# Block pairs' seven products in another order: four with rows of the first half of the tokens, then three of the second

## The chip, the cores and the metric

The kernel runs on one core of one Trainium2 chip. The metric is the device time of one execution in microseconds. Three runs of the kernel before gave 1287.32, 1287.40 and 1286.79 us, median 1287.32.

## The reference

One layer of a streaming encoder over 576 tokens (512 of a new stream, 64 of a running one), in float32. What matters here are the two feed-forward layers and the output projection of branch B.

```python
def swiglu_ffn(x, w_gate_up, w_down):
    gate, up = jnp.split(x @ w_gate_up, 2, axis=-1)
    return (jax.nn.silu(gate) * up) @ w_down
...
x = x + 0.5 * swiglu_ffn(rms_norm(x, ffn1_norm), ffn1_w_gate_up, ffn1_w_down)
...
y_b = b_act @ w_b_out
...
x = x + 0.5 * swiglu_ffn(rms_norm(x, ffn2_norm), ffn2_w_gate_up, ffn2_w_down)
```

The model width is 1024 and the hidden width 2816, that is 22 hidden tiles of 128.

## The kernel before

Features lie on the 128 partitions, the tokens on the free axis, in two halves of 288. Every float32 operand of a product is split into a high part (rounded to the format that TensorE multiplies at full rate) and a low part (the rest), and a product is three matmuls: high by high, high by low, low by high.

Most hidden tiles are computed as block pairs. The gate and the up weights of a hidden tile (in branch B two neighbouring output tiles), cut along the contraction into two parts of four tiles, and the two halves of the tokens form a 2 by 2 block product. It is done with seven products instead of eight, in Winograd's form: `plan_block` plans the weights, among them four sums s1 to s4 of weight blocks; `Forms` makes the sums t1 to t4 of the activations; `operands` lists the activations in the order of the products. A product (`block`) is 12 matmuls of 288 columns, into one bank of PSUM. Two products that follow each other share a PSUM tile of two banks (`bank`, line 171); the pool has four such tiles, and the pairing of banks runs on from pair to pair until `spare.clear()` at the end of a group. There are 41 block pairs: 18 in ffn1, 21 in ffn2 and 2 in branch B. In the feed-forward layers they stand in groups (four groups a layer, of one to six pairs), and a group ends with the down projection of its hidden tiles; the first two down tiles run interleaved (`both`).

TensorE multiplies an operand of the first half of the tokens or of the second. The halves start at addresses that differ by 128 bytes modulo 256, and `ws.places` puts the high and low parts of a product's weights at matching offsets: `(SHIFT, 0)` for products of the second half, `(0, SHIFT)` for those of the first.

The weights come through `Stream`. Each product has a unit; `lead` (called by `get` ahead of each product) works ahead by six units. For a unit it makes a sum if one is due (`add`, VectorE), writes the high part (`begin`, ScalarE) and the low part: VectorE subtracts it (`end`), or, for `how == "dma"`, ScalarE writes minus the high part and POOL issues a DMA that adds the raw weights to it. In a pair the units on a11, a12 and a22 go the second way in nearly all cases, the four sums the first. The raw weights are loaded by SP into six buffers.

While product n + 1 is issued, `steps[n]` combines what product n has given: `q1` is a copy of product 0 by ScalarE, `u2`, `u3` and `u4` are sums on VectorE, `t` becomes the gate and `cu` the up part. `gate` multiplies `t` by `R`, the reciprocal root of the norm, and ScalarE takes the Silu. `up`, `hidden` and `parts` of a pair run with the first products of the next (`rest`). Each engine keeps the order in which the code issues its instructions (`Ordered`). All of their instructions are issued through one helper, line 90.

Of the kernel before, what the change touches and what calls it, by code (L numbers as in the profile page):

```python
# [22 lines left out]
KU = KT // 2  # L23
# [90 lines left out]
def tile_encoder_step(  # L114
# [66 lines left out]
    def half(ap, s):  # L181
        return ap[:, s * H : (s + 1) * H]
# [176 lines left out]
    def plan_block(name, raws, homes, lows=("dma", "dma", "dma")):  # L359

        a21, a22, a11, a12 = raws
        s1, s2, s3, s4 = ((name, n) for n in range(1, 5))
        plan[name] = [
            ws.unit(src, KU, home, how, sums)
            for home, (src, how, sums) in zip(homes, (
                (a11, lows[0], ((s1, (a21, a22)),)),
                (s2, "dve", ((s2, (s1, a11)),)),
                (s1, "dve", ()),
                (s3, "dve", ((s3, (a11, a21)),)),
                (a12, lows[1], ()),  # L370
                (s4, "dve", ((s4, (s2, a12)),)),
                (a22, lows[2], ()),
            ))
        ]
        for n, unit in enumerate(plan[name]):
            second = n in (1, 5, 6)
            ws.places[unit] = (SHIFT, 0) if second else (0, SHIFT)

    def plan_ffn(f, gu, dn):
# [295 lines left out]
    class Forms:  # L675
# [25 lines left out]
        def operands(self, xg):  # L701

            first, second = (
                [(half(hi, s), half(lo, s)) for hi, lo in xg] for s in range(2)
            )
            t1, t2, t3, t4 = (
                [(half(hi, s), half(lo, s)) for hi, lo in (self.parts[p][i] for p in range(KU))]
                for i in range(2) for s in range(2)
            )
            return first[:KU], t2, t1, t3, first[KU:], second[KU:], t4  # L710


    ss = Sum()
# [140 lines left out]
    def ffn(f, xg, sums, finish, forms, R=None, todo=()):  # L854
        todo = list(todo)

        rest = []


        def plain(i, hs):  # L860
            nonlocal R
            t, up = ttile(), (f, "u", i)
            ps = product((f, "g", i), xg, order=IN_TURN if f == "f2" and i == 0 else None)
            got = None if up in early else chunks(up)
            if R is None:
                R = rstd(sums)
            ups = product(up, xg, got=got)
            hs.append(None)
            at = len(hs) - 1

            def gate():
                dve.tensor_tensor(halves(t), ps, halves(R), op=ALU.mult)
                sca.activation(t, t, AF.Silu)

            def hidden():
                dve.tensor_tensor(halves(t), ups, halves(t), op=ALU.mult)
                hs[at] = high(t)

            def parts():
                hs[at] = hs[at], low(t, hs[at])  # L880

            if f == "f2":
                rest.extend((gate, hidden, parts))
                return
            gate()
            forming()
            hidden()
            forming()
            parts()
            forming()  # L890

        def forming():
            if todo:
                for step, p in todo.pop(0):
                    step(p)

        def pair(i, hs, last):
            qu, uu, t, cu = (ttile() for _ in range(4))
            q1, u2, u3, u4 = half(qu, 0), half(qu, 1), half(uu, 0), half(uu, 1)
            q = []  # L900

            def q7():
                dve.tensor_tensor(u3, q[3], u2, op=ALU.add)
                dve.tensor_tensor(half(cu, 1), u3, q[2], op=ALU.subtract)

            def gate():
                dve.tensor_tensor(half(t, 1), q[5], u4, op=ALU.add)
                dve.tensor_tensor(t, t, R, op=ALU.mult)
                sca.activation(t, t, AF.Silu)

            steps = (
                lambda: sca.copy(q1, q[0]),
                lambda: dve.tensor_tensor(u2, q[1], q1, op=ALU.subtract),
                lambda: dve.tensor_tensor(u4, q[2], u2, op=ALU.subtract),
                q7,
                lambda: dve.tensor_tensor(half(t, 0), q[4], q1, op=ALU.add),
                gate,
            )
            for n, xs in enumerate(bs):
                q.append(block(ws.get(plan[f, "s", i][n]), xs))  # L920
                if n > 0:
                    steps[n - 1]()
                if rest:
                    rest.pop(0)()

            hs.append(None)
            at = len(hs) - 1

            def up():
                if last:  # L930
                    dve.tensor_tensor(t, t, R, op=ALU.mult)
                dve.tensor_tensor(half(cu, 0), q[6], u3, op=ALU.add)

            def hidden():
                dve.tensor_tensor(cu, cu, t, op=ALU.mult)
                hs[at] = high(cu)

            def parts():
                hs[at] = hs[at], low(cu, hs[at])

            rest.extend((up, hidden, parts))

        for g, grp in enumerate(GROUPS):
            hs = []
            for i in grp:
                if i < PLAIN[f]:
                    plain(i, hs)
                    continue
                if i == PLAIN[f]:
                    ws.ahead = AHEAD_UNITS  # L950
                    bs = forms.operands(xg)
                pair(i, hs, grp[-1] == FT - 1)
            while rest:
                rest.pop(0)()
            spare.clear()
            if grp[-1] < FT - 1:
                for j, ps in enumerate(both([(f, "d", g, j) for j in range(2)], hs, turn=True)):
                    update(j, ps, R)
                for j in range(2, KT):
                    update(j, product((f, "d", g, j), hs), R)  # L960
            else:
                finish(g, hs)
# [315 lines left out]
    def block_pair(i):  # L1278
# [2 lines left out]
        q1, u2, u3, u4 = half(qu, 0), half(qu, 1), half(uu, 0), half(uu, 1)  # L1281
        q = []

        def second():
            dve.tensor_tensor(u3, q[3], u2, op=ALU.add)
            dve.tensor_tensor(half(c2, 1), u3, q[2], op=ALU.subtract)

            if i == KU - 1:
                MS[4], MS[5] = split(M[4]), split(M[5])

        def first():
# [1 line left out]
            dve.tensor_tensor(c1, c1, SGB[j], op=ALU.mult)  # L1293
            merged(j, c1)

        steps = (
            lambda: sca.copy(q1, q[0]),
            lambda: dve.tensor_tensor(u2, q[1], q1, op=ALU.subtract),
            lambda: dve.tensor_tensor(u4, q[2], u2, op=ALU.subtract),
            second,  # L1300
            lambda: dve.tensor_tensor(half(c1, 0), q[4], q1, op=ALU.add),
            first,
        )
        for n, xs in enumerate(bs):
            q.append(block(ws.get(plan["yb", "s", i][n]), xs))
            if n > 0:
                steps[n - 1]()
        dve.tensor_tensor(half(c2, 0), q[6], u3, op=ALU.add)
        dve.tensor_tensor(c2, c2, SGB[j + 1], op=ALU.mult)
# [166 lines left out]
```

## Time and profile before

| | |
|---|---|
| median of three runs | 1287.32 us |
| profiled execution | 1287.41 us |
| its span | 1285.6 us |
| granted TensorE clock, mean | 0.998 |
| TensorE busy | 1275.0 us, 99% |
| VectorE busy | 927.8 us, 72% |
| ScalarE busy | 762.8 us, 59% |
| POOL busy | 357.2 us, 28% |
| matmuls | 9728 |
| 41 block pairs, 11.05 us each | about 453 us |

The page gives busy time per engine as a share of the span and, in another part, the chain of work that ended last. A matmul's row shows its whole passage (293 ns on the mean) although the next one starts 0.13 us later, so the distance between starts says more than the duration. A row of the list in order of time has the start in us, the duration, the engine, the line, what is written and read, and, in brackets, how long the engine was idle before it and who ended that. `PE` is TensorE, `DVE` VectorE, `ACT` ScalarE.

### The profile page before, as it was taken

To read this page: it belongs to the slowest core of one execution; us is meant where nothing else is said; L and a number is where in the kernel's file an instruction comes from. 1 tells how busy PE (TensorE), PEld (TensorE's weight loads), DVE (VectorE), ACT (ScalarE), POOL (GpSimd) and SP (SyncE) were. 2 spreads that over 40 slices of the span, in tenths; PEclk is the share of its full clock that TensorE was granted. 3 is DMA by queue.
4 is the path that set the end of the run, shared out by engine and by line. 5 is a ranking of instruction groups with operands and counts; after the bars stand their busy time and mean duration, and the time that the engine had idled before them with its cause. 6 is when DMAs were issued, how large, how long until landed. Compare 5 with 4: busy or idle time off the path is not lost.

```text
span 1285.6 us, 25688 instructions
## 1 busy us (share of the span) xinstructions
PE 1275.0 (99%) x9728; PEld 1273.3 (99%) x9728; DVE 927.8 (72%) x1544; ACT 762.8 (59%) x1354; POOL 357.2 (28%) x455
## 2 busy tenths in 40 slices
PE   9999999999999999999999999999999999999997
PEld 9999999999999999999999999999999999999996
DVE  6868668748846998888895166756967848847955
ACT  7645646646776645555444576467665655654664
POOL 0032332332333444333321221122142141241230
PEclk9999999999999999999999999999999999999999
DMA  7287786886799898878885767686597696796693
GB/s 222 69 181 154 164 181 154 178 183 147 157 225 230 173 207 166 172 168 177 169 169 124 170 137 160 147 207 147 132 177 174 147 203 147 165 207 140 153 181 93
DMA packets 286091, 213.94 MB, mean 166 GB/s; under 512 B 15376, under 2 KB 248848, under 8 KB 285968
## 3 DMA queue, kind: packets, MB, share of 16 engines
q0 software_dynamic: 55440, 91.12, 43.3%
q1 hardware_dynamic: 228784, 120.35, 32.9%
q8 instruction: 77, 1.26, 0.4%
q10 hardware_dynamic: 1744, 0.83, 0.2%
q14 instruction: 46, 0.38, 0.1%
HBM read 116.17 MB, written 4.98 MB: 94 GB/s over the span
## 4 chain that ended last, share of the span: by engine, by line
PE 98%; DMA 1%; DVE 0%; ACT 0%; SPq 0%; DVEq 0%; issue 0%
PE mm L90 98%; DMA x<-in_x_dram 0%; DMA gains<-in_params_dram 0%; DVE g L90 0%; DVE tmp L90 0%; SPq L730 0%; DVE act L90 0%; ACT act L90 0%; DVEq L1466 0%; DVE r L90 0%; DVE x L90 0%; ACT tmp L90 0%; ACT r L90 0%
## 5 line engine op out<-in xcount | busy, mean ns | idle before, releaser
L90 PE MATMUL mm<-act,u 128*128 128x288 f32 x4758 | 666.2, 293 | 0.0
L90 PEld LDWEIGHTS mm<-act,u 128*128 128x128 f32 x4758 | 637.2, 188 | 0.0
L90 PE MATMUL mm<-act,g 128*128 128x288 f32 x3030 | 431.5, 293 | 0.0
L90 PEld LDWEIGHTS mm<-act,g 128*128 128x128 f32 x3030 | 408.9, 188 | 0.3 <-DMA g<-raw 0.2
L90 POOL DMA_DIRECT2D u<-raw x194 | 169.3, 873 | 477.1 <-ACT u L90 311.6
L90 PE MATMUL mm<-act,act 128*128 128x288 f32 (+2 forms) x1896 | 258.8, 293 | 0.5 <-DVE act L90 0.3
L90 PEld LDWEIGHTS mm<-act,act 128*128 128x128 f32 x1896 | 251.1, 188 | 1.1 <-DVE act L90 0.6
L90 ACT CAST u<-raw 128x512 fp32r<-128x512 f32 (+2 forms) x207 | 118.9, 575 | 172.3 <-PE mm L90 142.0
L90 POOL DMA_DIRECT2D g<-raw x124 | 107.8, 869 | 302.5 <-ACT g L90 246.4
L90 DVE SCALAR_TENSOR_TENSOR w<-g,prm,w 128x606 f32<-128x606 f32 x232 | 179.3, 842 | 1.4 <-ACT w L90 1.4
L90 DVE TENSOR_TENSOR tmp<-mm,tmp 128x288 f32<-128x288 f32 (+1 forms) x251 | 112.7, 457 | 67.3 <-PE mm L90 50.9
L90 ACT ACTIVATE u<-u 128x512 fp32r<-128x512 f32 (+2 forms) x194 | 115.0, 593 | 6.2
L90 ACT CAST g<-raw 128x512 fp32r<-128x512 f32 (+2 forms) x136 | 75.1, 552 | 45.6 <-DMA raw<-in_ffn_w_down_dram 16.3
L90 DVE SCALAR_TENSOR_TENSOR tmp<-mm,r 128x576 f32<-128x576 f32 x48 | 36.3, 756 | 74.8 <-PE mm L90 74.8
L90 POOL DMA_DIRECT2D act<-raw x67 | 59.1, 883 | 107.9 <-ACT act L90 94.2
L90 ACT CAST act<-tmp 128x576 fp32r<-128x576 f32 x92 | 61.9, 675 | 43.6 <-DVE tmp L90 42.5
L90 ACT CAST g<-w 128x512 fp32r<-128x512 f32 x79 | 49.0, 620 | 63.4 <-DVE w L90 55.8
L90 ACT CAST u<-w 128x512 fp32r<-128x512 f32 x81 | 50.2, 619 | 59.5 <-DVE w L90 43.3
L90 DVE TENSOR_TENSOR act<-tmp,act 128x576 fp32r<-128x576 f32 x92 | 67.5, 754 | 18.4 <-ACT act L90 16.8
L90 ACT ACTIVATE g<-g 128x512 fp32r<-128x512 f32 (+2 forms) x124 | 70.9, 572 | 3.9
L90 DVE TENSOR_TENSOR w<-raw,raw 128x512 f32<-128x512 f32 x82 | 56.1, 684 | 16.6 <-DMA raw<-in_ffn_w_gate_up_dram 12.1
L90 ACT ACTIVATE tmp<-tmp 128x576 f32<-128x576 f32 x47 | 32.2, 685 | 44.1 <-DVE tmp L90 44.1
(86 smaller groups left out, 833.4 us busy)
## 6 DMA issues: line engine op xcount, KB each, us to landing
raw<-in_ffn_w_gate_up_dram SPq DMA_DIRECT2D x171, 256.0 KB, 3.4
u<-raw POOLq DMA_DIRECT2D x137, 256.0 KB, 4.1
raw<-in_w_in_dram SPq DMA_DIRECT2D x112, 256.0 KB, 3.9
raw<-in_ffn_w_down_dram SPq DMA_DIRECT2D x96, 192.0 KB, 3.8
g<-raw POOLq DMA_DIRECT2D x67, 256.0 KB, 4.0
act<-raw POOLq DMA_DIRECT2D x61, 256.0 KB, 4.3
g<-raw POOLq DMA_DIRECT2D x43, 192.0 KB, 4.5
u<-raw POOLq DMA_DIRECT2D x41, 192.0 KB, 4.5
```

The source lines that it names most:

```text
L90: return self.tc.keep_in_program_order(fn(*args, **kwargs))
```

## The change

The products of a pair come in another order. Before: a11, s2, s1, s3, a12, s4, a22; after: a11, s1, s3, a12, s2, s4, a22. In the first order products 1, 5 and 6 multiply rows of the second half of the tokens, in the second one products 4, 5 and 6. The combining steps follow: nothing is computed behind products 1 and 2; `t`'s first half comes behind product 3, and u2, u4, u3 and the lower half of `cu` together behind product 4 (`middle`). In branch B the splits of `M[4]` and `M[5]` go with them.

```diff
             for home, (src, how, sums) in zip(homes, (
                 (a11, lows[0], ((s1, (a21, a22)),)),
-                (s2, "dve", ((s2, (s1, a11)),)),
                 (s1, "dve", ()),
                 (s3, "dve", ((s3, (a11, a21)),)),
                 (a12, lows[1], ()),
+                (s2, "dve", ((s2, (s1, a11)),)),
                 (s4, "dve", ((s4, (s2, a12)),)),
                 (a22, lows[2], ()),
             ))
...
-            second = n in (1, 5, 6)
+            second = n >= 4
             ws.places[unit] = (SHIFT, 0) if second else (0, SHIFT)
...
-            return first[:KU], t2, t1, t3, first[KU:], second[KU:], t4
+            return first[:KU], t1, t3, first[KU:], t2, second[KU:], t4
...
-            def q7():
-                dve.tensor_tensor(u3, q[3], u2, op=ALU.add)
-                dve.tensor_tensor(half(cu, 1), u3, q[2], op=ALU.subtract)
+            def middle():
+                dve.tensor_tensor(u2, q[4], q1, op=ALU.subtract)
+                dve.tensor_tensor(u4, q[1], u2, op=ALU.subtract)
+                dve.tensor_tensor(u3, q[2], u2, op=ALU.add)
+                dve.tensor_tensor(half(cu, 1), u3, q[1], op=ALU.subtract)
...
-            steps = (
-                lambda: sca.copy(q1, q[0]),
-                lambda: dve.tensor_tensor(u2, q[1], q1, op=ALU.subtract),
-                lambda: dve.tensor_tensor(u4, q[2], u2, op=ALU.subtract),
-                q7,
-                lambda: dve.tensor_tensor(half(t, 0), q[4], q1, op=ALU.add),
-                gate,
-            )
+            steps = {
+                0: lambda: sca.copy(q1, q[0]),
+                3: lambda: dve.tensor_tensor(half(t, 0), q[3], q1, op=ALU.add),
+                4: middle,
+                5: gate,
+            }
             for n, xs in enumerate(bs):
                 q.append(block(ws.get(plan[f, "s", i][n]), xs))
-                if n > 0:
+                if n - 1 in steps:
                     steps[n - 1]()
```

`block_pair` (branch B) changes in the same way.

VectorE's order in one pair of ffn1, before. `act` is the low half of the previous hidden tile, `mm` are products (two share a number), `w` are sums of weights, `g` and `u` the low parts of weights; `tmp_3094` holds q1 and u2, `tmp_3095` u3 and u4, `tmp_3096` is t, `tmp_3097` is cu:

```order
L90 TENSOR_TENSOR tmp_3094<-mm_3112,tmp_3094 128x288
L90 TENSOR_TENSOR act_3165<-tmp_2948,act_3146 128x576
L90 TENSOR_TENSOR g_3149<-w_3126,g_3148 128x512
L90 TENSOR_TENSOR w_3168<-raw_3019,raw_2958 128x512
L90 TENSOR_TENSOR tmp_3095<-mm_3151,tmp_3094 128x288
L90 TENSOR_TENSOR u_3172<-w_3099,u_3172 128x512
L90 TENSOR_TENSOR tmp_3095<-mm_3151,tmp_3094 128x288
L90 TENSOR_TENSOR tmp_3097<-tmp_3095,mm_3151 128x288
L90 TENSOR_TENSOR g_3189<-w_3168,g_3188 128x512
L90 TENSOR_TENSOR w_3207<-w_3126,raw_3106 128x512
L90 TENSOR_TENSOR tmp_3096<-mm_3191,tmp_3094 128x288
L90 TENSOR_TENSOR tmp_3096<-mm_3191,tmp_3095 128x288
```

The same engine and pair now:

```order
L90 TENSOR_TENSOR act_3166<-tmp_2948,act_3144 128x576
L90 TENSOR_TENSOR g_3151<-w_3099,g_3150 128x512
L90 TENSOR_TENSOR u_3169<-w_3146,u_3169 128x512
L90 TENSOR_TENSOR w_3184<-w_3099,raw_2999 128x512
L90 TENSOR_TENSOR tmp_3096<-mm_3153,tmp_3094 128x288
L90 TENSOR_TENSOR w_3205<-w_3184,raw_3106 128x512
L90 TENSOR_TENSOR tmp_3094<-mm_3191,tmp_3094 128x288
L90 TENSOR_TENSOR tmp_3095<-mm_3112,tmp_3094 128x288
L90 TENSOR_TENSOR tmp_3095<-mm_3153,tmp_3094 128x288
L90 TENSOR_TENSOR tmp_3097<-tmp_3095,mm_3112 128x288
L90 TENSOR_TENSOR u_3207<-w_3184,u_3207 128x512
L90 TENSOR_TENSOR tmp_3096<-mm_3191,tmp_3095 128x288
```

u2, which stood ahead of the low half `act`, and u4 have moved behind product 4 (`mm_3191`), in one run of four operations with u3 and cu.

ScalarE's order in the same pair, before, from the Silu on (`CAST` writes a high part, the `ACTIVATE` behind it minus the high part for a DMA, `COPY` is q1):

```order
L90 ACTIVATE tmp_2947<-tmp_2947 128x576
L90 CAST g_3101<-raw_2810 128x512
L90 ACTIVATE g_3102<-g_3101 128x512
L90 CAST u_3128<-raw_3019 128x512
L90 ACTIVATE u_3128<-u_3128 128x512
L90 COPY tmp_3094<-mm_3112 128x288
L90 CAST act_3146<-tmp_2948 128x576
L90 CAST g_3148<-w_3126 128x512
L90 CAST u_3172<-w_3099 128x512
L90 CAST g_3188<-w_3168 128x512
L90 CAST u_3209<-raw_3106 128x512
L90 ACTIVATE u_3209<-u_3209 128x512
```

And now:

```order
L90 ACTIVATE tmp_2947<-tmp_2947 128x576
L90 CAST g_3101<-raw_2810 128x512
L90 ACTIVATE g_3102<-g_3101 128x512
L90 CAST u_3126<-raw_2999 128x512
L90 ACTIVATE u_3126<-u_3126 128x512
L90 COPY tmp_3094<-mm_3112 128x288
L90 CAST act_3144<-tmp_2948 128x576
L90 CAST g_3150<-w_3099 128x512
L90 CAST u_3169<-w_3146 128x512
L90 CAST g_3186<-raw_3106 128x512
L90 ACTIVATE g_3187<-g_3186 128x512
L90 CAST u_3207<-w_3184 128x512
```

The first seven stand where they stood; a12 (`raw_3106`) has moved ahead of a sum.

More of the change, by code (lines that the diff above doesn't have):

```diff
@@ L1282, in block_pair, with middle @@
         q = []
-        def second():
-            dve.tensor_tensor(u3, q[3], u2, op=ALU.add)
-            dve.tensor_tensor(half(c2, 1), u3, q[2], op=ALU.subtract)
+        def middle():
+            dve.tensor_tensor(u2, q[4], q1, op=ALU.subtract)
+            dve.tensor_tensor(u4, q[1], u2, op=ALU.subtract)
+            dve.tensor_tensor(u3, q[2], u2, op=ALU.add)
+            dve.tensor_tensor(half(c2, 1), u3, q[1], op=ALU.subtract)
             if i == KU - 1:
@@ L1294, in first @@
             merged(j, c1)
[L1296 to L1303, printed above, removed]
+        steps = {
+            0: lambda: sca.copy(q1, q[0]),
+            3: lambda: dve.tensor_tensor(half(c1, 0), q[3], q1, op=ALU.add),
+            4: middle,
+            5: first,
+        }
         for n, xs in enumerate(bs):
             q.append(block(ws.get(plan["yb", "s", i][n]), xs))
-            if n > 0:
+            if n - 1 in steps:
                 steps[n - 1]()
```

## The prediction

> **What bounds the kernel now.** I read the page first, then the chain that ended last, then one pair's instructions in order of time on each engine, then single DMA issues.
>
> ```profile
> span 1285.6 us, 25688 instructions
> ...
> PE 1275.0 (99%) x9728; PEld 1273.3 (99%) x9728; DVE 927.8 (72%) x1544; ACT 762.8 (59%) x1354; POOL 357.2 (28%) x455
> ...
> PE 98%; DMA 1%; DVE 0%; ACT 0%; SPq 0%; DVEq 0%; issue 0%
> ```
>
> TensorE is the chain: 98% of the span, one matmul behind the other. So an edit can gain only by making matmuls follow each other more closely, and it can lose by making TensorE wait for a weight or a bank. The profiled execution took 1287.41 us: its span of 1285.6 and 1.8 around it. The median is 1287.32, so I take 0.1 off at the end. A measurement of this kernel tells about 0.2% (2.6 us) from no change.
>
> TensorE's rows of one pair in ffn2, the third of its group (start, us, then what; twelve matmuls a product; I number the products 0 to 6):
>
> ```profile
> 1002.70 1.75 PE L90 MATMUL mm<-act,g 128*128 128x288 f32 x12
> ...
> 1007.44 1.74 PE L90 MATMUL mm<-act,u 128*128 128x288 f32 x12
> 1009.01 1.74 PE L90 MATMUL mm<-act,g 128*128 128x288 f32 x12
> ...
> 1012.17 1.74 PE L90 MATMUL mm<-act,g 128*128 128x288 f32 x12
> 1013.75 0.42 PE L90 MATMUL mm<-act,u 128*128 128x288 f32 x2
> ```
>
> From start to start a pair takes 11.05 us, a product 1.58, a matmul 0.131. Only product 3 (1007.44 to 1009.01, 1.57) has neighbours on both sides that multiply the same half of the tokens. TensorE does not wait within the pair.
>
> VectorE's rows there. `tmp<-tmp,r` is the step in `gate` that multiplies by R; I call its start the R step. The row 1007.53 is u2, 1008.10 the low half of the previous hidden tile, 1010.95 and 1011.43 are u3 and the lower half of cu, 1013.01 the two halves of t:
>
> ```profile
> 1003.38 0.76 DVE L90 TENSOR_TENSOR tmp<-tmp,r 128x576 f32<-128x576 f32 x1
> ...
> 1007.53 0.46 DVE L90 TENSOR_TENSOR tmp<-mm,tmp 128x288 f32<-128x288 f32 x1 [0.55 <-ACT tmp L90]
> 1008.10 0.76 DVE L90 TENSOR_TENSOR act<-tmp,act 128x576 fp32r<-128x576 f32 x1
> 1008.78 0.69 DVE L90 TENSOR_TENSOR g<-w,g 128x512 fp32r<-128x512 f32 x1
> ...
> 1010.95 0.45 DVE L90 TENSOR_TENSOR tmp<-mm,tmp 128x288 f32<-128x288 f32 x1
> 1011.43 0.45 DVE L90 TENSOR_TENSOR tmp<-tmp,mm 128x288 f32<-128x288 f32 x1
> 1011.80 0.68 DVE L90 TENSOR_TENSOR g<-w,g 128x512 fp32r<-128x512 f32 x1
> 1012.40 0.68 DVE L90 TENSOR_TENSOR w<-w,raw 128x512 f32<-128x512 f32 x1
> 1013.01 0.81 DVE L90 TENSOR_TENSOR tmp<-mm,tmp 128x288 f32<-128x288 f32 x2
> 1013.85 0.76 DVE L90 TENSOR_TENSOR tmp<-tmp,r 128x576 f32<-128x576 f32 x1
> ```
>
> VectorE goes from one R step to the next in 10.47 us with hardly a gap, in a pair of 11.05: it is almost a second bound. Start to start, an operation that needs the one before it follows after 0.48 (1010.95 to 1011.43), one that doesn't after 0.37 (1011.43 to 1011.80), one behind 512 columns after 0.60 (1011.80 to 1012.40), one behind the low half after 0.68.
>
> The R step drives the rest. ScalarE waits for it with the Silu, and behind the Silu stand in its queue the splits of two weights that a DMA on POOL finishes:
>
> ```profile
> 1004.18 0.69 ACT L90 ACTIVATE tmp<-tmp 128x576 f32<-128x576 f32 x1 [1.47 <-DVE tmp L90]
> 1007.39 0.68 ACT L90 CAST act<-tmp 128x576 fp32r<-128x576 f32 x1
> 1006.33 0.86 POOL L90 DMA_DIRECT2D g<-raw  x1 [4.30 <-DVE w L90]
> 1007.50 0.86 POOL L90 DMA_DIRECT2D u<-raw  x1 [0.31 <-ACT tmp L90]
> ```
>
> From the R step it is 0.80 to the Silu, 2.95 and 4.12 to the two DMAs (a22 of this pair, a11 of the next), 4.01 to the high half of the hidden tile and 4.72 (1008.10) to its low half. A later R step makes these weights later by as much.
>
> **The change: what it saves.** A pair's seven products change the half of the tokens four times before (into 1, into 2, into 5, into the next pair) and twice after. Four changes touch eight product ends. With 1.57 for a product without one, 7 x 1.57 = 10.99, and the 0.06 left to 11.05 over eight ends is 0.0075 an end, so two changes less are 0.03 us a pair. The rows round to 10 ns, which leaves 0.01 to 0.05. The starts behind them, read to the nanosecond, give 1.5733 for that product and 11.054 for the pair, which is 0.005 an end and 0.021 a pair. I take 0.021: 41 pairs x 0.021 = 0.85 us, with 0.4 and 2.0 as ends.
>
> The Trainium skill's page "TensorE: Matmul & The Clock Gate" (Part 2, step by step) says that TensorE has two independent read ports in SBUF, and that loading the next weights takes no bandwidth from the running matmul. By that rule the half of the tokens would not matter, the saving would be 0 instead of 0.85, and the sum below 1290.2. The rows above disagree by a hundredth of a microsecond a product, and the measurement decides.
>
> **What it moves.** The number of instructions stays, and so do their sizes: the same four sums, splits and DMAs a pair, seven combining operations, loads on SP in the same order. SP's loads are not moved past anything; the a12 load must be there one product earlier, and ScalarE reaches a12 only 5.7 us behind the R step, and waits for no load there in the rows of before: I cost it nothing. On POOL the a12 DMA comes one earlier in the pair, with its product, behind the same two DMAs: nothing. Banks: product 1 is now held until product 4 is done; the first products behind a group that ends on an odd pair reuse those of products 2 and 3, which are read 0.05 us before they are needed. I cost that nothing and keep 0.5 us for five such places as an end.
>
> What costs is VectorE's order. u2 and u4, which stood in the slack behind products 1 and 2, now stand behind product 4 with u3 and cu. Two things follow.
>
> First, u2 waits for more. Two products share a PSUM tile, and an operation that is issued behind the next product waits for that one too, if it writes the same tile. Two rows show this:
>
> ```profile
> 990.06 1.74 PE L90 MATMUL mm<-act,g 128*128 128x288 f32 x12
> 990.27 0.82 DVE L90 TENSOR_TENSOR tmp<-mm,tmp 128x288 f32<-128x288 f32 x2
> 991.12 0.76 DVE L90 TENSOR_TENSOR tmp<-tmp,r 128x576 f32<-128x576 f32 x1
> 1018.76 0.46 DVE L90 TENSOR_TENSOR tmp<-mm,tmp 128x288 f32<-128x288 f32 x1 [1.31 <-PE mm L90]
> ```
>
> In the first pair of that group, and every second one from there (call them odd), products 4 and 5 share a tile: the step on product 4 started at 990.27, just when product 5 had ended (product 6 starts at 990.06), and the R step came 0.85 later. The pair began 6 x 1.58 earlier, at 980.59, so its R step is at 10.5. In the even pairs 1 and 2 share one, and u2 there waited 1.31 us for product 2 (1018.76; the pair starts at 1013.75). After the change u2 stands where the step on product 4 stood: in odd pairs it starts at 9.68 at the earliest, then u4 0.48, u3 0.37, cu 0.48, a weight's low half 0.37, t 0.60, the R step 0.48 later: 9.68 + 2.78 = 12.46 us into the pair.
>
> Second, VectorE's loop gets longer: 4.72 from the R step to the low half, then 0.68 + 0.60 + 0.60 + 0.60 (two low halves, a sum, t's first half) + 0.37 + 0.60 (a sum, u2) + 2.78 = 10.95, against 10.47. That is still 0.1 below the 11.03 of a pair, so the even pairs' R step is at 12.46 + 10.95 - 11.03 = 12.37 and the odd ones keep 12.46.
>
> **Where this reaches TensorE.** At the end of a group the first weights of the second down tile are read ten matmuls, 1.31 us, behind the last pair; their DMA follows the R step of the last pair but one. There are seven such ends with DMAs. The first, the tightest and the costliest (R step; POOL issue; its landing; TensorE's first matmul behind the pair):
>
> ```profile
> 144.01 0.76 DVE L90 TENSOR_TENSOR tmp<-tmp,r 128x576 f32<-128x576 f32 x1
> 150.49 0.86 POOL L90 DMA_DIRECT2D g<-raw  x1
> g<-raw POOLq DMA_DIRECT2D x1, 192.0 KB, 4.5
> 154.37 2.40 PE L90 MATMUL mm<-act,g 128*128 128x288 f32 x17
> 939.45 0.76 DVE L90 TENSOR_TENSOR tmp<-tmp,r 128x576 f32<-128x576 f32 x1
> 945.92 0.86 POOL L90 DMA_DIRECT2D g<-raw  x1
> g<-raw POOLq DMA_DIRECT2D x1, 192.0 KB, 4.2
> 948.72 3.06 PE L90 MATMUL mm<-act,g 128*128 128x288 f32 x20
> 1122.48 0.76 DVE L90 TENSOR_TENSOR tmp<-tmp,r 128x576 f32<-128x576 f32 x1
> 1129.17 0.86 POOL L90 DMA_DIRECT2D u<-raw  x1
> u<-raw POOLq DMA_DIRECT2D x1, 192.0 KB, 4.8
> 1133.42 2.81 PE L90 MATMUL mm<-act,u 128*128 128x288 f32 x20
> ...
> u<-raw POOLq DMA_DIRECT2D x137, 256.0 KB, 4.1
> ...
> u<-raw POOLq DMA_DIRECT2D x1, 256.0 KB, 5.9
> ```
>
> - 154.37: the weights land at 154.99, read at 155.68: 0.69 to spare. The R step (two pairs before the end, so 144.01 - 154.37 + 22.11 = 11.75) moves to 12.37: 0.62 later, no stall.
> - 948.72: they land at 950.12 and should be read at 950.03: nothing to spare. The R step there is at 12.84; this group comes late out of the mixer, and before it catches up by 11.05 - 10.47 a pair, which the longer loop no longer does. Two loops of 10.95 for 10.47 make it 0.96 later; in one of the two pairs a22 is split without a DMA, which by ScalarE's rows shortens the way by about 0.1. I take 0.84, all of it stall.
> - 1133.42: 0.76 to spare, the R step from 11.17 to 12.46: 1.29 later, 0.53 of stall.
> - The other four, read in the same way: 1.45, 0.79, 0.75 and 0.91 to spare, 1.30, 1.01, 0.63 and 1.00 later: stalls of 0, 0.22, 0 and 0.09.
>
> Together 1.7 us. Inside the groups a22 and a11 have 5.1 to 5.6 us left from issue to use at the new R step; by the page such a landing takes 4.1 at the median (the last row but one above), but the last row, of a DMA issued at 325.9, took 5.9. The three latest of this trace would stall TensorE by 0.56, 0.18 and 0.08 (that one landed at 331.82 for a read at 332.32, and its R step moves by 1.01; a start follows a landing by 0.05): 0.8 us. The terms are lopsided, since a landing that is later by a few tenths stalls and an earlier one gains nothing; for the six places within 0.2 of the edge I add 0.3.
>
> Sum: -0.85 + 1.7 + 0.8 + 0.3 = +1.95 us, 1289.4 for the profiled execution, **1289.3** beside the median. That is +0.15%.
>
> **Rivals.**
> 1. The margins hold, and only the saving is left: 1287.3 - 0.85 = 1286.5. For it: six of the seven ends have 0.7 us or more. Against it: the wait of u2 for product 5 is sure, and two ends are short by half a microsecond even at median landings.
> 2. Slower: VectorE's loop becomes longer than TensorE's pair. Place: the four chained operations behind product 4. It decides at 11.03 us; I have 10.95, from intervals that each round by 0.01 and of which two (u2 to u4, u4 to u3) no row shows in this order. At 11.3 every pair but the first two of a group slips by 0.27, some 27 pairs, 7 us, of which the spare 0.7 us in each of seven groups is swallowed: +2.1 on top of the other stalls, 1291.4.
> 3. The change of half costs more than the rows say and the gain exceeds 0.2%. That takes 63 ns a pair, twice what the pair has beyond 7 x 1.57 for two changes. Nearly excluded.
> 4. The change of half costs nothing, the 1.57 being a rounding, and only the stalls are left: 1289.3 + 0.85 = 1290.2. For it: the rows differ by one unit of their last place. Against it: the nanosecond starts. The Trainium skill's rule on the two ports, named above, is on this side.
>
> **How the numbers follow.** Stalls outweigh the saving: 0.55, own range 1288.0 to 1291.0. Only the saving: 0.18. The loop slips: 0.19. The change of half costs nothing: 0.05. More than 0.2% gained: 0.03. Slower by over 0.2% starts at 1289.9: a third of the first case (0.19), all of the loop's and half of the fourth make about 0.41; faster 0.03; the same 0.56. The range goes from 1286.4, the second case, to 1292.2, the loop's at 11.33.
>
> **What would show it.** Right: an R step at about 12.4 in both kinds of pair, VectorE's u2 behind the end of product 5, no product with two changes of half, 11.03 us a pair, and TensorE waiting some tenths at 950 and 1134 for a DMA on POOL. Wrong: R steps that drift from pair to pair (rival 2), or no TensorE wait near those places (rival 1), or products behind odd pairs that start late for a bank.

## The result, and the profile after

The changed kernel takes 1300.12 us (median of six runs, 1295.34 to 1301.27) beside 1287.45 of the kernel before (six runs, 1286.79 to 1288.41): 1.0095 times as long, with a 95% interval from 1.0085 to 1.0106. The prediction was 1289.3, with a range up to 1292.2. It was wrong. In the rounds of the experiments below the kernel before also took 1290.6 to 1297.8 us in ten of 82 runs, at the same granted clock; none of the ten was profiled.

The page of after:

```profile
span 1298.7 us, 25748 instructions
...
PE 1283.9 (99%) x9728; PEld 1280.5 (99%) x9728; DVE 931.2 (72%) x1544; ACT 760.6 (59%) x1354; POOL 357.5 (28%) x455
...
PE 91%; issue 3%; DVE 2%; DMA 2%; ACT 1%; POOL 0%; SPq 0%; DVEq 0%; ACTq 0%; POOLq 0%
```

TensorE is still 99% busy, with 8.9 us more of it (1275.0 before), and has left the chain in several places (98% before, 91% now).

The same pair as in the prediction, the third of its group in ffn2, in order of time. TensorE, first product of this pair and of the next:

```profile
1012.49 1.74 PE L90 MATMUL mm<-act,g 128*128 128x288 f32 x12
...
1023.52 1.74 PE L90 MATMUL mm<-act,u 128*128 128x288 f32 x12
```

VectorE; the first and the last row are the R step of the second pair (which began at 1001.45) and of the third, 1022.14 holds u2, u4 and u3, 1023.49 is the lower half of cu:

```profile
1013.85 0.76 DVE L90 TENSOR_TENSOR tmp<-tmp,r 128x576 f32<-128x576 f32 x1
...
1022.14 1.32 DVE L90 TENSOR_TENSOR tmp<-mm,tmp 128x288 f32<-128x288 f32 x3
1023.49 0.46 DVE L90 TENSOR_TENSOR tmp<-tmp,mm 128x288 f32<-128x288 f32 x1
1023.86 0.68 DVE L90 TENSOR_TENSOR u<-w,u 128x512 fp32r<-128x512 f32 x1
1024.46 0.45 DVE L90 TENSOR_TENSOR tmp<-mm,tmp 128x288 f32<-128x288 f32 x1
1024.95 0.76 DVE L90 TENSOR_TENSOR tmp<-tmp,r 128x576 f32<-128x576 f32 x1
```

The pair takes 11.03 us (11.05 before), and the R step comes 12.40 us into the even pair and 12.46 into the odd one, without drift. Inside the pairs all is as forecast. The loss lies elsewhere.

TensorE's waits. Five of them, on TensorE's rows:

```profile
132.98 1.19 PE L90 MATMUL mm<-act,g 128*128 128x288 f32 x7 [0.71 <-DMA g<-raw]
154.97 1.80 PE L90 MATMUL mm<-act,g 128*128 128x288 f32 x12
358.61 1.57 PE L90 MATMUL mm<-act,g 128*128 128x288 f32 x10 [0.26 <-DMA g<-raw]
826.55 1.69 PE L90 MATMUL mm<-act,u 128*128 128x288 f32 x11 [1.38 <-DVE tmp L90]
1251.26 1.98 PE L90 MATMUL mm<-act,u 128*128 128x288 f32 x13 [1.88 <-DMA u<-raw]
```

A bracket counts from the modelled end of the last matmul, so I take the distance of the starts less the usual 0.131. Added up that way, TensorE waits 7.1 us in after and 0.3 in before: 4.8 us for late DMAs on POOL (the two longest 2.15 at 1251.26 and 0.98 at 132.98), 2.3 us for VectorE at five places where a product takes a bank that VectorE still reads (1.62 at 826.55; 0.16 to 0.17 at 154.97 and three other places).

The larger part is no wait. The plain products (all outside the block pairs) run at another rate. One window in the mixer, the part between the two feed-forward layers, from behind the twelve turned matmuls (explained below) at its first root to its second root, the same 2192 matmuls; a root is a place where four matmuls with `ones_r` give the sum that R or its like is made from; the columns are the window, its length, TensorE's busy time, the granted clock, the share of the DMA engines and GB/s. Before:

```profile
401.59:686.29 284.70, 284.70 (x2192) 1.00 0.84 176
```

After:

```profile
403.71:692.06 288.35, 288.35 (x2192) 1.00 0.83 173
```

The change does not touch this code, TensorE never waits in it, the clock is full in both, and it takes 3.65 us more. Two rows of plain products in it (24 matmuls between starts), before and after:

```profile
453.08 3.28 PE L90 MATMUL mm<-act,u 128*128 128x288 f32 x24
456.20 3.28 PE L90 MATMUL mm<-act,act 128*128 128x288 f32 x24
```

```profile
455.86 3.32 PE L90 MATMUL mm<-act,u 128*128 128x288 f32 x24
459.02 3.32 PE L90 MATMUL mm<-act,act 128*128 128x288 f32 x24
```

3.12 us before, 3.16 now: six matmuls of a plain product (one k tile; below "a six") take 780 ns before and 790 after, in code that did not change. Counted from the starts to the nanosecond, behind the first 27 us: before has 854 sixes at 780, 103 at 790 and 12, inside turned products, near 807; after has 98, 860 and 3, and eight that hold a wait. Over 780 a six that is 1.4 us in before and 9.1 in after, 7.7 more.

So the account is 6.8 of waits + 7.7 of slower plain products - 0.85 saved in the pairs = 13.6 us; between 27 us and the last turned product the traces differ by 13.3.

What changes the rate in before is visible as well. `turned`, and `both` with `turn=True`, run twelve matmuls in another order. In before each stretch behind block pairs begins at 790 and goes over to 780 at the turn, but for one: behind ffn2's first group, at 950, where before has its one longer wait (0.26 us), the 39 sixes behind the turn stay at 790. So the turns stand where an undisturbed stream needs them.

### The profile page after: what moved, and what is told of

Same layout as the page of the kernel before. It is cut to its first block, busy times and chain, and to the rows that moved or that the text cites. A ratio compares the mean times of both kernels' runs of the same rounds, so it can differ in the third digit from the quotient of the medians.

```text
span 1298.7 us, 25748 instructions
## 1 busy us (share of the span) xinstructions
PE 1283.9 (99%) x9728; PEld 1280.5 (99%) x9728; DVE 931.2 (72%) x1544; ACT 760.6 (59%) x1354; POOL 357.5 (28%) x455
## 4 chain that ended last, share of the span: by engine, by line
PE 91%; issue 3%; DVE 2%; DMA 2%; ACT 1%; POOL 0%; SPq 0%; DVEq 0%; ACTq 0%; POOLq 0%
PE mm L90 91%; DVE tmp L90 1%; DMA g<-raw 1%; DVE g L90 0%; DMA u<-raw 0%; ACT g L90 0%; ACT u L90 0%; DMA raw<-in_w_b_out_dram 0%; DVE u L90 0%; DMA raw<-in_ffn_w_gate_up_dram 0%; DVE w L90 0%; ACT act L90 0%; ACT tmp L90 0%; DVE x L90 0%; DVE act L90 0%
## 5 line engine op out<-in xcount | busy, mean ns | idle before, releaser
L90 DVE TENSOR_TENSOR w<-raw,raw 128x512 f32<-128x512 f32 x82 | 55.7, 685 | 18.8 <-DMA raw<-in_ffn_w_gate_up_dram 13.3
```

The costliest lines, as they stand in the source:

```text
L90: return self.tc.keep_in_program_order(fn(*args, **kwargs))
```

## The experiments

Theory A: a late step makes TensorE wait at the end of a group; a wait leaves TensorE at another rate than the undisturbed stream has there; and the turns, right for that stream, then set 790 for hundreds of products. Rival B: the loss is waits alone. Rival C: the order of the products sets the rate of the plain products behind them.

**The rate alone: a turn taken out.** From both kernels the same line goes:

```diff
             R = rstd(ss)
-            turning[0] = True
```

In the kernel before:

> The kernel before without the one turned product behind the first root of the mixer; nothing else changes, and no engine waits for anything new. In the trace of before, six matmuls of a plain product on one pair of activation tiles take 780 ns in most stretches and 790 ns in others, and a turned product stands where 790 goes over to 780. Theory A (TensorE keeps one of two rates until something switches it; this, not waits alone, is where the time went): the 365 sixes from 401.6 us to 686.3 us run at 790 instead of 780, +3.7 us, and if the next two turns then switch the wrong way, 147 more, +1.5: 1291.0 to 1292.7 us. Rival B (the loss is waits alone, the rates are a by-product): 1287.4 us, within 1.

Measured: 1292.15 us median (1288.07 to 1293.89), ratio 1.0037, 1.0023 to 1.0051. But the run with the profile was the one at 1288.07, and showed the mixer at 780 and the 52 sixes ahead of it at 790:

```profile
402.46:687.16 284.70, 284.70 (x2192) 1.00 0.84 176
```

So it was run again, for another profile:

> The kernel before without the first turned product of the mixer, again, for another profile: its five times were 1288.07 (the one with the profile, where the 52 sixes ahead of the mixer ran at 790 and the mixer at 780) and 1291.08 to 1293.89. Theory A: a run near 1292 shows 780 in those 52 and 790 in the mixer, 365 or 512 sixes; a run near 1288 shows what the first profile shows. Rival B: a run near 1292 shows waits of 4 us and no more sixes at 790.

Measured: 1293.12 us. The same window in this profile:

```profile
401.22:689.57 288.35, 288.35 (x2192) 1.00 0.82 174
```

Now the 52 sixes ahead ran at 780, and the mixer takes the 288.35 of after to the last digit, in the kernel before, with the old order of products. 544 sixes at 790 beside 103 are 4.3 us; two late landings of this run are 1.3 us more. Rival B falls: a rate is worth 3.65 us in one window without a wait. That the two profiles differ shows that the rate at a place is not fixed from run to run. Two things stand ahead of it in them. In the first profile one product, at 332.36 and more than two pairs ahead of the 52 sixes, took 1.69 us instead of 1.58, the only such place between 27 and 400 us; the second has none there. And between 28 and 57 us, where no pair has run yet and TensorE waits in neither, 36 sixes ran at 790 in the first and at 780 in the second.

In the changed kernel:

> The changed kernel without the same turned product. Its trace shows 790 ns a six from 403.7 us to 850 us, where before has 780. Theory A: the 366 sixes up to 693.9 us now run at 780, -3.7 us, and if the next two turns keep it so, 163 more, -1.7: 1294.7 to 1296.4 us beside 1300.1. Rival B: 1300.1 us, within 1.

Measured: 1295.63 us (1295.18 to 1298.18), ratio 1.0067, 1.0052 to 1.0082, 4.5 below the changed kernel, as theory A had it. The window:

```profile
404.57:689.27 284.70, 284.70 (x2192) 1.00 0.83 176
```

The mixer is back at 284.70, with the new order of products and with all its waits (6.6 us). The same line taken out makes one kernel slower and the other faster. The sixes around the four roots say why. Without a turned product behind it, a root swaps the two rates: 780 ahead becomes 790 behind, and 790 becomes 780. So it is in these three profiles at the first root, and in all sixteen of this document, where 780 or 790 stands ahead, at the fourth (ahead of ffn2's pairs), which never has a turn. With a turned product the rate ahead comes back behind it, at every root and in every profile where it was 780 or 790. So the turned product swaps the rates once more, and the mixer inherits what the end of ffn1 left: 780 in before, 790 in after.

**The combining steps issued earlier.**

```diff
-                4: middle,
...
                 q.append(block(ws.get(plan[f, "s", i][n]), xs))
+                if n == 4:
+                    middle()
```

(in `block_pair` too)

> The changed order of products, with u2, u4, u3 and cu issued before product 5 instead of behind it, so that u2 waits for product 4 alone. The R step should come at 10.6 us into a pair instead of 12.4. Theory A: the waits at the group ends for VectorE and for late weights go away except for a landing that is late by itself (0 to 1.5 us), nothing switches TensorE's rate any more, and the plain products run at 780 as before: 1287.4 - 0.85 + 0 to 1.5 = 1286.5 to 1288.1 us. Rival C (the order of the products itself sets the rate of the plain products behind them): the waits' 6.5 us are gone, the slow rate's 7.6 us stays: 1292.9 to 1294.5 us. Rival B: 1286.5 to 1288.1 us with any rate.

Measured: 1312.52 us (1312.01 to 1313.74). All of the expected times were missed, and the two questions get separate answers. The rate: 927 sixes at 780, 30 at 790, so rival C falls; no group end makes TensorE wait. Its waits inside pairs, 26 us in all, leave the rate as it is, so not every wait changes a rate. The time: every pair whose products 4 and 5 share a PSUM tile takes 11.92 us instead of 11.03. TensorE's rows of products 4 and 5 of such a pair:

```profile
1026.94 1.74 PE L90 MATMUL mm<-act,g 128*128 128x288 f32 x12
1029.32 1.81 PE L90 MATMUL mm<-act,u 128*128 128x288 f32 x12 [0.64 <-DVE tmp L90]
```

Product 5 starts 2.38 behind product 4 instead of 1.58: it writes the tile that u2 reads, and u2 now stands ahead of it in the program. Behind product 5, u2 waits for TensorE; ahead of it, TensorE waits for u2.

**Old order, late steps.** The kernel before, with nothing behind products 1 to 3, and t's first half, u2, u4, u3 and cu behind product 4:

```diff
+            def fourth():
+                dve.tensor_tensor(half(t, 0), q[4], q1, op=ALU.add)
+                middle()
...
+            steps = {
+                0: lambda: sca.copy(q1, q[0]),
+                4: fourth,
+                5: gate,
+            }
```

> The old order of products and halves, but with the combining steps of the new one: nothing behind products 1 to 3, and behind product 4, issued behind product 5, t's first half and then u2, u4, u3 and cu. The R step should come at 12.4 to 12.9 us into a pair. Theory A (the late steps make the waits, the waits switch the rate): waits of 6 to 10 us at the group ends, and 790 ns in more than half of the sixes, so 1296 to 1303 us. Rival C (the product order sets the rate): the waits alone, with 780 ns nearly everywhere as in before: 1293.5 to 1297.5 us.

Measured: 1306.34 us (1303.46 to 1308.06), more than either theory gave; 13.6 us of waits and 802 sixes at 790. The late steps alone, without the new order, cost all that the changed kernel lost, and more. VectorE's loop is longer here; R steps of three pairs of ffn1's last group:

```profile
314.21 0.76 DVE L90 TENSOR_TENSOR tmp<-tmp,r 128x576 f32<-128x576 f32 x1
...
325.70 0.76 DVE L90 TENSOR_TENSOR tmp<-tmp,r 128x576 f32<-128x576 f32 x1
...
337.20 0.76 DVE L90 TENSOR_TENSOR tmp<-tmp,r 128x576 f32<-128x576 f32 x1
```

11.49 apart, in pairs of 11.05: the drift that the prediction's second rival described, in another kernel.

**Other PSUM tiles for the products.** First, each pair begins a new tile, and so does product 5: (0,1), (2,3), (4), (5,6).

```diff
             for n, xs in enumerate(bs):
+                if n in (0, 5):
+                    spare.clear()
                 q.append(block(ws.get(plan[f, "s", i][n]), xs))
```

With the early steps:

> The changed order, u2, u4, u3 and cu issued before product 5 as in the run with the early steps, and now each pair begins with a new PSUM tile and products 4 and 5 lie in different tiles: (0,1), (2,3), (4), (5,6). In the run with the early steps alone every second pair, the ones whose products 4 and 5 share a tile, took 11.92 us instead of 11.03, and the plain products ran at 780 ns a six in 928 of 969. Theory A (product 5 waited there for u2 to read the shared tile; late steps make the waits, waits switch the rate): all pairs at 11.03, the R step at 10.6 to 10.8, no waits at the group ends but for single late landings, 780 ns nearly everywhere: 1285.7 to 1286.8 us. Rival D (the 0.89 us a pair is VectorE's loop, which with an idle stretch ahead of u2 is longer than 11.03): pairs of 11.2 to 11.9, 1295 to 1312 us.

Measured: 1286.97 us (1286.58 to 1287.83), ratio 0.9989, 0.9974 to 1.0004. In five rounds more:

> The early steps with products 4 and 5 in different tiles, again, in more rounds: three rounds gave 1286.97 us beside 1287.52, a ratio of 0.9989 with an interval that reaches 1.0004. If the saving of 0.021 us a pair (0.85 us) is all that is left between the two, 1286.4 to 1287.0 us and a ratio of 0.9993 to 0.9997; if it is lost in late landings that differ from run to run, 1.0000 or more.

Measured: 1287.74 us (1286.14 to 1288.68) beside 1287.49, ratio 1.0001, 0.9992 to 1.0010. Over both it is level with the kernel before, a little over theory A's range (up to 1286.8). The page of the second run:

```profile
span 1285.6 us, 25752 instructions
...
PE 1275.0 (99%) x9728; PEld 1273.5 (99%) x9728; DVE 931.4 (72%) x1544; ACT 761.1 (59%) x1354; POOL 356.9 (28%) x455
...
PE 98%; DMA 1%; DVE 0%; ACT 0%; issue 0%; DVEq 0%; POOLq 0%
```

That is the page of before almost line by line, and the counts of sixes are those of before (854, 103, 12). Six pairs of ffn1's last group take 66.20 us instead of 66.32, so the saving of 0.020 a pair is there. One wait is left, in ffn2's first group:

```profile
948.71 1.35 PE L90 MATMUL mm<-act,g 128*128 128x288 f32 x9
950.43 1.74 PE L90 MATMUL mm<-act,g 128*128 128x288 f32 x11 [0.37 <-DMA g<-raw]
```

The layout alone, with the steps behind product 5 as in the changed kernel:

> The changed kernel with that layout of PSUM tiles alone; u2, u4, u3 and cu stay behind product 5 in the order of issue. Theory A (what made the R step late in the changed kernel is u2's wait for product 5 in the shared tile, in the first pair of a group, from which VectorE's loop of 10.95 us cannot catch up): the R step at 10.6 to 11.0, hardly a wait at the group ends, 780 ns nearly everywhere, 1285.7 to 1288 us. Rival E (the lateness is the length of VectorE's work, not the shared tile): R step at 12 or later, a wait for cu at each pair's first product on top, 1300 us or more.

Measured: 1288.40 us (1287.55 to 1290.01), ratio 0.9997, 0.9980 to 1.0014. Two added lines (in `pair` and in `block_pair`) take 11.7 us off the changed kernel. The time is a little over theory A's range, 893 sixes are at 780, and 2.5 us of waits are left. But the R step stands at 11.7 and not at 10.6. I put that down to products 5 and 6 sharing a tile, and moved product 6 to the next pair's product 0, (1,2), (3,4), (5), (6,0), by clearing at products 1, 5 and 6:

> The changed kernel with another layout of PSUM tiles alone: (1,2), (3,4), (5), and product 6 with product 0 of the next pair; the order of issue stays. In the two runs where products 5 and 6 shared a tile the R step stood at 11.72 and 11.86 in every pair, 0.7 to 0.8 behind product 6's end, and the theory had said 10.6. Theory A, mended (each combining step waits for the later product of the tile it reads, and that alone sets the R step): R step at 10.4 to 10.9, so the waits that run kept behind branch B (0.7), in ffn2's first group (0.9) and at the last group end (0.6) shrink to 0 to 0.5 together, 780 ns in over 890 sixes: 1285.6 to 1287.0 us. Rival E (VectorE's work of 10.95 a pair sets it): R step stays near 11.7 and the time at 1288.4.

> The same layout, and u2, u4, u3 and cu issued before product 5. Here products 3 and 4 share a tile and 5 has one of its own, so product 5 has not to wait for u2. Theory A: pairs at 11.03, R step at 10.4 to 10.7, at most one wait in ffn2's first group, 1285.5 to 1286.7 us, within 0.5 of the run without the early steps. Rival E: an idle stretch ahead of u2 lengthens VectorE's loop beyond 11.03: pairs of 11.1 or more, 1290 us or more.

Measured: 1287.56 us (1287.22 to 1293.56, ratio 1.0003, 0.9992 to 1.0014) with the late steps, 1287.72 us (1287.20 to 1288.82) with the early ones, 0.6 and 1.0 over theory A's ranges. The first of them on TensorE (the first product of a pair and of the next) and on VectorE (1011.48 is t's first half, 1012.45 u2, u4 and u3, 1013.79 cu, the last row the R step):

```profile
1003.40 1.74 PE L90 MATMUL mm<-act,g 128*128 128x288 f32 x12
...
1014.43 1.74 PE L90 MATMUL mm<-act,u 128*128 128x288 f32 x12
```

```profile
1010.82 0.68 DVE L90 TENSOR_TENSOR w<-w,raw 128x512 f32<-128x512 f32 x1
1011.48 0.46 DVE L90 TENSOR_TENSOR tmp<-mm,tmp 128x288 f32<-128x288 f32 x1
1011.86 0.68 DVE L90 TENSOR_TENSOR w<-w,raw 128x512 f32<-128x512 f32 x1
1012.45 1.31 DVE L90 TENSOR_TENSOR tmp<-mm,tmp 128x288 f32<-128x288 f32 x3
1013.79 0.46 DVE L90 TENSOR_TENSOR tmp<-tmp,mm 128x288 f32<-128x288 f32 x1
1014.17 0.69 DVE L90 TENSOR_TENSOR u<-w,u 128x512 fp32r<-128x512 f32 x1
1014.77 0.45 DVE L90 TENSOR_TENSOR tmp<-mm,tmp 128x288 f32<-128x288 f32 x1
1015.25 0.76 DVE L90 TENSOR_TENSOR tmp<-tmp,r 128x576 f32<-128x576 f32 x1
```

The R step is at 11.85, so my reading of the tiles of 5 and 6 was wrong. t's first half starts 8.08 into the pair, 0.66 behind the row ahead of it, where 0.60 is usual: it waited for product 4, which had ended 0.2 behind the start of product 5 (at 1011.28), because product 3, which it reads, now shares a tile with 4. From there to R VectorE works for 3.77 us without a gap. A floor of 11.7 to 11.9 is therefore set by the work behind product 4, as rival E had it for the R step; the last 0.5 to 0.7 us, up to 12.4, came from u2's wait for product 5. That half microsecond decides most of the waits at the group ends: with 12.4 TensorE waits at all nine, with 11.7 (the layout alone) at two.

**Waits put into the kernel before.** VectorE writes one column of the tile of the first down product, behind its R step of the last pair, at the four ends of ffn1:

```diff
-            while rest:
-                rest.pop(0)()
             spare.clear()
+            ps = [psum2() for _ in range(2)]
+            if f == "f1":
+                dve.tensor_copy(ps[0][:, 0, :1], eps)
+            while rest:
+                rest.pop(0)()
```

> The kernel before with one small wait at each of the four group ends of ffn1: VectorE writes one column into the PSUM tile of the first down product behind its R step of the last pair, so TensorE should wait 0.3 to 0.6 us there for VectorE, 1.2 to 2.4 us in all; nothing else changes. Theory A (a wait switches TensorE's rate, and the turns behind it, made for the undisturbed stream, then set it wrong): behind some of the four ends 790 instead of 780 ns a six; 36, 36, 44 and 51 sixes hang on the four, and 512 of the mixer on the last: over 150 sixes at 790 and 1290 to 1296 us. Rival B (a wait costs its length): 1288.6 to 1289.9 us and some 105 sixes at 790 as in before.

Measured: 1299.60 us (1299.04 to 1300.52), ratio 1.0084, 1.0058 to 1.0109. The waits were longer than planned, 5.7 us in all, and 705 sixes ran at 790. Four waits in the kernel before (which also takes the first two down products' tiles a little earlier, at all eight ends) make 12.1 us, nearly the whole loss of the changed kernel, 6.1 us of it by rate. The same without the turned products at these four ends:

> The kernel before with the four small waits at ffn1's group ends, and without the turned products behind them. With the turns it took 1299.6 us: four waits of 5.6 us in all, and 716 sixes at 790. Theory A: the waits stay, the rate is 780 in most sixes behind them and in the mixer: 1292.5 to 1294.5 us. Rival F (the wait alone makes the stretch behind it slow): 1299 to 1301 us.

Measured: 1295.18 us (1293.80 to 1295.50), ratio 1.0050, 1.0033 to 1.0066; 4.4 us less with the same waits. The last of the four ends, with turns and then without them (the last column counts the matmuls of a row):

```profile
362.18 4.95 PE L90 MATMUL mm<-act,g 128*128 128x288 f32 x36 [1.51 <-DVE mm L90]
366.97 3.32 PE L90 MATMUL mm<-act,u 128*128 128x288 f32 x24
```

```profile
361.00 5.07 PE L90 MATMUL mm<-act,g 128*128 128x288 f32 x36 [1.51 <-DVE mm L90]
365.91 5.00 PE L90 MATMUL mm<-act,u 128*128 128x288 f32 x36
370.75 1.51 PE L90 MATMUL mm<-act,g 128*128 128x288 f32 x10
```

With the turn, the first two sixes behind the wait took 780 and those behind the turn 790. Without it the rows give 4.84 for 36, 807 a six: a third rate, which before does not show outside its turned products. The four waits of this run were followed by 790, 790, 780 and 807. So a wait does not set a rate that can be counted on.

**The turns taken out at eight ends of the changed kernel.**

> The changed kernel without the turned products at eight places: the ends of ffn1's groups except the third, the output projection and all ends of ffn2; the three turns inside the mixer stay. All waits of the changed kernel stay (6.8 us more than before by its trace). Its trace has 871 sixes at 790 where before has 105. Theory A (at each of these ends the wait has already switched the rate and the turn switches it back): 100 to 300 sixes at 790, so 5.8 to 7.8 us less than 1300.1: 1292.3 to 1294.3 us. Rival F (a late VectorE or late DMA slows the plain products by itself, whatever the turns): still over 700 sixes at 790 and 1299 to 1301 us.

Measured: 1298.80 us (1294.35 to 1301.57), ratio 1.0077, 1.0048 to 1.0106. The profile belongs to the run of 1301.57: 772 sixes at 790 and 113 near 807, although the turns are gone. Theory A misses the time by 4.5 us. Rival F of this expectation (a late step slows the products behind it by itself) has its count met and its time missed by 0.2 us, but it had given 1299 to 1301 us for the four waits without turns too, where 1295.18 came. The half of theory A which says that the turn behind a wait is wrong and without it all is well falls: behind these waits the stream stood at 790 or 807 by itself.

**One turn less in the best version**, behind ffn2's first group (`turn=(f, g) != ("f2", 0)`):

> The same without the turned product behind the first group of ffn2. In its trace that place had the one wait left (a landing at 949.75 us), and the 39 sixes behind it ran at 790. Theory A (the wait had switched the rate already, so that the turn set it wrong): 780 there, 0.4 us less than the run beside it, 1286.0 to 1286.6 us. If the wait comes in some runs and not in others: the same time as the run beside it, within 0.2, with a wider spread.

Measured: 1287.38 us (1286.49 to 1289.07), ratio 1.0001: no gain. The sixes behind the wait ran near 807 in its profile, and TensorE waited 1.3 us at the last group end. No version here beats the kernel before by more than a measurement tells.

**The accounts.** Differences to before in us, each from its one profile, from 27 us to the last turned product. Rate: what the sixes take over 780 each. Pairs: 41 x 0.021 where the new order stands.

| kernel | waits | rate | pairs | sum | measured |
|---|---|---|---|---|---|
| changed | 6.8 | 7.7 | -0.85 | 13.6 | 13.3 |
| changed, no mixer turn | 6.3 | 2.9 | -0.85 | 8.4 | 8.2 |
| changed, eight turns out | 6.0 | 9.7 | -0.85 | 14.8 | 14.5 |
| before, no mixer turn (second run) | 1.3 | 4.3 | 0 | 5.7 | 5.7 |
| before, four waits | 5.7 | 6.1 | 0 | 11.8 | 11.7 |
| before, four waits, no turns there | 5.3 | 1.8 | 0 | 7.1 | 7.1 |
| before, late steps | 13.2 | 7.3 | 0 | 20.5 | 20.2 |
| early steps, own tiles (second run) | 0.3 | 0.0 | -0.85 | -0.5 | -0.5 |

Two terms and the saving account for every kernel of the table within 0.4 us. The rate term of the changed kernel holds a piece of luck: between 28 and 57 us, ahead of the first pair, 36 sixes ran at 780 in its profile and at 790 in before's, 0.4 us in its favour.

## Why the prediction was wrong

- **The saving** was right: 0.021 us a pair forecast, 66.317 less 66.197 over six is 0.020. In after's ffn2 the products 1, 2 and 5 of a pair, which now have the same half on both sides, take 1.573 each, as product 3 did in before.
- **VectorE's order** was right: the R step at 12.46 and 12.40 (forecast 12.46 and 12.37), a loop of 10.97 (10.95), no drift. The second rival did not come about.
- **The waits for POOL's DMAs** were forecast at 1.7 + 0.8 + 0.3 = 2.8 and are 4.5 more than before, but not where they were forecast. The costliest, 0.84 at 948.72, did not come: the R steps of that group's first three pairs stand at 13.58, 13.14 and 12.76 (13.83, 13.47 and 12.89 before), not at 13.8 in the third, and TensorE waits 0.25 there as in before (0.26), and 0.31 at 925.63 inside the group. The 0.53 at 1133.42 came out at 0.24. The step that failed is that a landing keeps its duration. The weights for 1251.26 had 0.91 to spare and were to be 1.00 later, "stalls of 0, 0.22, 0 and 0.09"; but their DMA, 4.4 us before, now took 6.2, and TensorE waited 2.15. Before and after:

```profile
1233.27 0.86 POOL L90 DMA_DIRECT2D u<-raw  x1
u<-raw POOLq DMA_DIRECT2D x1, 192.0 KB, 4.4
```

```profile
1244.99 0.86 POOL L90 DMA_DIRECT2D u<-raw  x1
u<-raw POOLq DMA_DIRECT2D x1, 192.0 KB, 6.2
```

  The 0.98 at 132.98, inside a group, is the same: a DMA of 3.9 us in before took 6.6. The DMA of the last group end took 5.4 to 6.2 in six of the sixteen profiles and 4.3 to 4.5 in the other ten. The moment of its issue alone does not decide it: own tiles and one turn less issued it 3.5 us ahead of the group's end, as own tiles alone did, and it took 5.9 there and 4.3 here. Why was not tried.
- **Banks**: "I cost that nothing and keep 0.5 us for five such places" failed. Four places cost 0.16 to 0.17 each, a little over the 0.1 each of that end of the range, the fifth, behind branch B's first pair, 1.62. VectorE's rows there, the first from before and the others from after:

```profile
816.11 0.69 DVE L90 TENSOR_TENSOR w<-raw,raw 128x512 f32<-128x512 f32 x1 [1.77 <-DMA raw<-in_w_b_out_dram]
```

```profile
823.52 0.69 DVE L90 TENSOR_TENSOR w<-raw,raw 128x512 f32<-128x512 f32 x1 [3.25 <-DMA raw<-in_w_b_out_dram]
824.13 0.45 DVE L90 TENSOR_TENSOR tmp<-mm,tmp 128x288 f32<-128x288 f32 x1
824.50 0.68 DVE L90 TENSOR_TENSOR g<-raw,g 128x512 fp32r<-128x512 f32 x1
825.10 1.30 DVE L90 TENSOR_TENSOR tmp<-mm,tmp 128x288 f32<-128x288 f32 x3
```

  VectorE stands 3.25 us at a sum of weights that have not landed. In before it stood there too (1.77, until 9.3 us into the pair; now 9.5), but u2 and u4 had been issued ahead of that sum. Now the whole run stands behind it, u3 ends at 826.4, and the product that needs its bank was due at 825.0. The prediction took the margin from the feed-forward layers and did not read branch B's own rows; that `block_pair` changes in the same way was its only thought on it.
- **The rate** is the step that failed most: "it can lose by making TensorE wait for a weight or a bank" takes a wait at its own length. There was no term for plain products that go on at another rate behind it: 7.7 us, more than all waits. The rows were there. Before's own trace had sixes at 780 and at 790 on the same kind of product, and a turned product at every change from 790 to 780. The code has `turned` and `turning` for no other purpose that the trace shows, and the prediction does not mention them.
- The rivals: none of the four gave over 1291.4. The last sentence of the prediction, "products behind odd pairs that start late for a bank", named the sign that came.

What is shown of the rate is this: it comes and goes without the new order, without any wait in the window, at full granted clock, and a root or a turned product swaps it. The Trainium skill's page "TensorE: Matmul & The Clock Gate" (Part 2, step by step) gives TensorE two independent read ports in SBUF, one for the streaming operand and one for the weights. By that alone the same matmuls would have one spacing; these runs show three, 780, 790 and 807 ns a six. What holds a stream at one of them, and what decides which one a wait leaves, stays open.

## What to carry to other kernels

A wait on a saturated engine can cost more than its length: compare the spacing of identical instructions ahead of it and behind it, over the whole rest of the trace, before a stall is priced. When steps are bunched behind one product, look for each tile that two products share and for each wait that now stands ahead of the bunch; two lines in each of two functions, which put products 4 and 5 into different PSUM tiles, gave back 11.7 of 12.7 us. And where a kernel has odd pieces of order that compute nothing, find out in the trace what they hold in place before moving anything ahead of them.

## What the hardware did that I had not expected

- The same six matmuls of one program took 780 ns in one execution and 790 in another, and stay so for hundreds of sixes; about 807 came too, for 38 to 71 sixes on end in three kernels. The 2192 matmuls took 284.70 or 288.35 us in eight profiles of seven kernels; the other eight profiles show nothing between either.
- A change of order within twelve matmuls (`turned`) takes the stream from 790 to 780, or from 780 to 790, and so do the four matmuls of a root.
- The DMA of 192 KB on POOL ahead of the last group end took 4.3 to 4.5 us in ten profiles and 5.4 to 6.2 in six.
